# One transfer for the first x and for y of step 6, six stores for the first result, and row sums moved between VectorE and ScalarE, in a softmax over the diagonal of a Gram matrix

## The chip, the core and the metric

The kernel runs on one core of a Trainium2 chip. The metric is the device time of one execution in microseconds, given as the median of several runs.

## The reference

```python
B, N, D = 8, 4096, 512           # x and y: float32, standard normal
gram = np.matmul(x, y.transpose(0, 2, 1))
diag = np.diagonal(gram, axis1=1, axis2=2)      # (8, 4096)
diag = diag - diag.max(axis=-1, keepdims=True)
exp = np.exp(diag)
return exp / exp.sum(axis=-1, keepdims=True)
```

Only the diagonal of the Gram matrix is used, so what is computed is one dot product of 512 elements for each of 8 x 4096 rows, x[b, n] with y[b, n], and a softmax over the 4096 of each batch. No matrix product is needed. The inputs are 2 x 67.1 MB, the output is 131 KB.

## The kernel before

**Tiling.** Four batches at a time fill the 128 partitions: each batch takes 32 partitions, and each partition holds 128 consecutive rows of it. So there are two sets of results, set 0 (batches 0 to 3) and set 1 (batches 4 to 7), each 128 x 128. A set is worked off in four steps of 32 rows per partition, which makes eight steps, t = 0 to 7. One step brings 8 MB of x and 8 MB of y (64 KB of each per partition). In this text x2 is the x of step 2, y6 the y of step 6, and so on.

**Buffers.** `xs` has two buffers (steps alternate), `ys` has one, `side` is a small tile for 6 rows of y. `diag` receives the dot products, `res` the softmax.

**Order.** The schedule is written by hand (`manual_schedule`): each engine carries out its instructions in the order of the code. All loads are issued by SP on one DMA queue (`load_x`, L63, and `load_y`, L66), x of a step ahead of y of that step. An issue waits until the readers of the buffer it overwrites are done. The built program gives the completions of its transfers eight semaphores in turn; an issue also waits, where that is still open, for the transfer eight places ahead of it, which had the same semaphore.

**Steps 0 to 5.** When y has landed, ScalarE copies its last K = 6 rows to `side` (L123), while VectorE multiplies the first 26 rows of x by y in place (`products`, L70, 128x13312). At the end of these two `ys` is free, and SP issues the next y. VectorE then multiplies the last 6 rows with `side` (L70, 128x3072) and adds up the first 30 rows of products in one reduction (`sums`, L73); ScalarE adds up the last W = 2 rows, one ACTIVATE with an accumulator for each (`sums_act`, L78). When all sums of step t are there, its x buffer is free, and SP issues x of step t + 2. In step 0 x comes in two transfers, 2 rows and 30 rows. After step 3 the softmax of set 0 is made (`exps`, `normalize`), its last part at the beginning of step 4.

**Step 6.** x6 comes in one transfer, y6 in two halves of 16 rows. Each half is multiplied (L70, 128x8192) when it is there. ScalarE adds up 24 rows, VectorE 8. `ys` rows 0 to 15 are free after the first product and rows 16 to 31 after the second; y of step 7 goes there.

**Step 7.** x and y come in pieces of 16, 8, 4, 2, 1 and 1 rows, called a to f here (the x of the last two rows comes in one piece, e). VectorE does product and sum of a row in one instruction (`dots`, L83). A maximum over all columns but the last two is taken ahead of the last two rows (`largest`, L97).

**The end.** SP stores set 0 in four pieces of 32 partitions (L156), behind all loads on its queue; the softmax of set 1 follows the last dot product and is stored from ScalarE's queue (L158).

Of the kernel before, what the change touches and what calls it, by code (L numbers as in the profile page):

```python
# [1 line left out]

# [5 lines left out]


@with_exitstack
def kernel(
    ctx: ExitStack,
    tc: tile.TileContext,
    x: bass.AP,
    y: bass.AP,
    out: bass.AP,
):
    nc = tc.nc
    ctx.enter_context(tc.manual_schedule())  # L20
    f32 = mybir.dt.float32
    Alu = mybir.AluOpType
    Act = mybir.ActivationFunctionType
    X = mybir.AxisListType.X
    B, N, D = x.shape
    P = nc.NUM_PARTITIONS
    G = 32
    Q = P // G
    C = N // G
    R = 32  # L30
    H = R // 2
    K = 6
    W = 2
    S = B // Q * (C // R)


    xv = x.rearrange("(s b) (j c) d -> s (b j) c d", b=Q, j=G)
    yv = y.rearrange("(s b) (j c) d -> s (b j) c d", b=Q, j=G)
    ov = out.rearrange("(s b) (j c) -> s (b j) c", b=Q, j=G)

    big = ctx.enter_context(tc.tile_pool(name="big", bufs=1))
    small = ctx.enter_context(tc.tile_pool(name="small", bufs=1))


    xs = [big.tile([P, R, D], f32, name=f"xs{i}") for i in range(2)]
    ys = big.tile([P, R, D], f32, name="ys")
    side = big.tile([P, K, D], f32, name="side")

    diag = [small.tile([P, C + i], f32, name=f"diag{i}") for i in range(B // Q)]
    res = [small.tile([P, C], f32, name=f"res{i}") for i in range(B // Q)]  # L50

    def columns(t, r0, n):
        c0 = t % (C // R) * R + r0
        return slice(c0, c0 + n)

    def rows(t, r0, n):
        return xs[t % 2][:, r0 : r0 + n, :]

    def dots_of(t, r0, n):
        return diag[t * R // C][:, columns(t, r0, n)]  # L60

    def load_x(t, r0, n):
        nc.sync.dma_start(out=rows(t, r0, n), in_=xv[t * R // C, :, columns(t, r0, n), :])  # L63

    def load_y(t, r0, n):
        nc.sync.dma_start(out=ys[:, r0 : r0 + n, :], in_=yv[t * R // C, :, columns(t, r0, n), :])  # L66

    def products(t, r0, n, yt):
        xt = rows(t, r0, n)
        nc.vector.tensor_tensor(out=xt, in0=xt, in1=yt, op=Alu.mult)  # L70

    def sums(t, r0, n):
        nc.vector.tensor_reduce(out=dots_of(t, r0, n), in_=rows(t, r0, n), axis=X, op=Alu.add)  # L73

    def sums_act(t, r0, n):
        for r in range(r0, r0 + n):
            row = xs[t % 2][:, r, :]
            nc.scalar.activation(out=row, in_=row, func=Act.Copy, accum_out=dots_of(t, r, 1))  # L78

    def dots(t, r0, n):  # L80
        for r in range(r0, r0 + n):
            xt = xs[t % 2][:, r, :]
            nc.vector.scalar_tensor_tensor(  # L83
                out=xt, in0=xt, scalar=1.0, in1=ys[:, r, :], op0=Alu.mult, op1=Alu.mult,
                accum_out=dots_of(t, r, 1),
            )

    def over_quadrant(name, column, op, negate=False):

        got = small.tile([P, 1], f32, name=name)  # L90
        nc.vector.tensor_reduce(  # L91
            out=got, in_=column.to_broadcast([P, G]), axis=X, op=op, negate=negate, apply_transpose=True
        )
        return got

    def largest(out, d):
        nc.vector.tensor_reduce(out=out, in_=d, axis=X, op=Alu.max)  # L97

    def exps(i, d):
        mxp = small.tile([P, 1], f32, name=f"mxp{i}")  # L100
        largest(mxp, d)
        nmx = over_quadrant(f"nmx{i}", mxp, Alu.max, negate=True)
        sump = small.tile([P, 1], f32, name=f"sump{i}")
        nc.scalar.activation(out=res[i], in_=diag[i][:, :C], func=Act.Exp, bias=nmx, scale=1.0, accum_out=sump)  # L104
        return sump

    def normalize(i, sump):
        total = over_quadrant(f"sum{i}", sump, Alu.add)
        rc = small.tile([P, 1], f32, name=f"rc{i}")
        nc.vector.reciprocal(out=rc, in_=total)  # L110
        nc.vector.tensor_single_scalar(out=res[i], in_=res[i], scalar=rc, op=Alu.mult)  # L111

    nc.vector.addr_align(128, offset=0, max_nops=0)
    nc.scalar.addr_align(128, offset=0, max_nops=0)

    for t in range(S - 2):
        if t == 0:
            load_x(t, 0, 2)  # L120
        load_x(t, 2 if t == 0 else 0, R - 2 if t == 0 else R)
        load_y(t, 0, R)
        nc.scalar.activation(out=side, in_=ys[:, R - K :, :], func=Act.Copy)  # L123
        if t == C // R:
            normalize(0, sump)
        products(t, 0, R - K, ys[:, : R - K, :])
        products(t, R - K, K, side)
        sums(t, 0, R - W)
        sums_act(t, R - W, W)
        if t == C // R - 1:  # L130
            sump = exps(0, diag[0])

    t = S - 2
    load_x(t, 0, R)
    for r0 in (0, H):
        load_y(t, r0, H)
        products(t, r0, H, ys[:, r0 : r0 + H, :])
    sums(t, R - H // 2, H // 2)
    sums_act(t, 0, R - H // 2)

    t += 1
    r0 = 0
    for n in (16, 8, 4, 2, 1, 1):
        if r0 < R - 1:
            load_x(t, r0, max(n, 2))
        load_y(t, r0, n)
        if r0 == R - 2:
            largest(diag[1][:, C:], diag[1][:, : C - 2])
        dots(t, r0, n)
        r0 += n  # L150

    met = small.tile([P, C - R], f32, name="met")
    nc.scalar.activation(out=met, in_=diag[1][:, : C - R], func=Act.Copy)  # L153

    for p, n in ((0, G), (G, G), (2 * G, G), (3 * G, G)):
        nc.sync.dma_start(out=ov[0, p : p + n, :], in_=res[0][p : p + n, :])  # L156
    normalize(1, exps(1, diag[1][:, C - 2 :]))
    nc.scalar.dma_start(out=ov[1], in_=res[1])  # L158


# [1 line left out]
_INS = ['x', 'y']  # L162
_OUTS = [((8, 4096), 'float32')]


# [23 lines left out]
```

## Time and profile before

| | |
|---|---|
| median of 3 runs | 320.69 us (320.68 to 320.96) |
| span of the profiled execution | 318.9 us |
| busy: VectorE, ScalarE | 244.7 us (77%), 42.0 us (13%) |
| read from HBM, written | 134.22 MB, 0.13 MB |
| mean rate over the span | 421 GB/s |
| products of 26 rows, L70 | 14.03 us |
| products of 6 rows, L70 | 3.35 us |
| products of 16 rows, L70 | 8.68 us |
| sum of 30 rows, of 8 rows, L73 | 16.15 us, 4.42 us |
| one row on ScalarE, L78 | 616 ns, and 186 ns to read the accumulator |
| one row in step 7, L83 | 686 ns, and 81 ns to read the accumulator |

The profile is of one execution. Its span runs from the first to the last instruction, so it is shorter than the measured time, which holds what lies around it. Instruction times are busy times; two neighbours on an engine overlap a little, which is why a row on ScalarE follows the one before it after 0.61 us. Transfers have a time from issue to landing, which includes the wait in the queue behind earlier ones; the records of single DMA packets have start, duration and size.

### The profile page before, as it was taken

The page shows a single profiled execution, that of the slowest core. Times are in us where ns is not written, and L with a number is a line of the kernel's source. Part 1 is how long each engine was busy: PE and PEld are TensorE (multiplying, and loading weights), DVE is VectorE, ACT ScalarE, POOL GpSimd, SP SyncE. Part 2 cuts the span into 40 slices and gives each one's busy share as a digit, 9 for nine tenths or more (in the row PEclk, how much of TensorE's full clock was granted, in tenths as well). Part 3 has the DMA queues.
Part 4 walks back from the last instruction along what each step waited for, and adds up shares of the span by engine and source line. Part 5 has one row for each costly group of instructions (what it writes and reads, how often), then busy time and mean ns, then how long its engine had stood idle before and what let it go on. Part 6 is the DMA issues. An engine that isn't in the chain of part 4 may idle for free.

```text
span 318.9 us, 304 instructions
## 1 busy us (share of the span) xinstructions
DVE 244.7 (77%) x96; ACT 42.0 (13%) x84; POOL 0.2 (0%) x4
## 2 busy tenths in 40 slices
DVE  0000069995899939999399994999949999996995
ACT  1000030100301003010120103000030100197000
POOL 0000000000000000000000000000000000000000
DMA  8989999999999999999999999999999899999993
GB/s 314 493 378 485 436 395 436 485 395 403 510 403 395 477 444 395 427 493 395 403 510 403 395 460 460 395 419 493 403 395 510 358 444 415 444 423 419 421 413 116
DMA packets 4226, 134.37 MB, mean 421 GB/s; under 512 B 512, under 2 KB 768, under 8 KB 1536
## 3 DMA queue, kind: packets, MB, share of 16 engines
q1 hardware_dynamic: 4080, 134.29, 97.8%
q10 hardware_dynamic: 144, 0.07, 0.1%
q14 instruction: 2, 0.02, 0.0%
HBM read 134.22 MB, written 0.13 MB: 421 GB/s over the span
## 4 chain that ended last, share of the span: by engine, by line
DMA 62%; DVE 35%; issue 2%; SPq 0%; ACT 0%; DVEq 0%
DMA ys<-in_y_dram 62%; DVE xs L70 30%; DVE diag L73 4%; DVE xs L83 0%; SPq L63 0%; DVE res L111 0%; DVE nmx L91 0%; DVE sum L91 0%; ACT res L104 0%; DVE rc L110 0%; DVE mxp L97 0%; DVEq L70 0%; SPq L66 0%; DVEq L83 0%
## 5 line engine op out<-in xcount | busy, mean ns | idle before, releaser
L70 DVE TENSOR_TENSOR xs<-xs,ys 128x13312 f32<-128x13312 f32 (+1 forms) x8 | 101.4, 12690 | 66.5 <-DMA ys<-in_y_dram 66.5
L73 DVE TENSOR_REDUCE diag<-xs 128x30 f32<-128x15360 f32 (+1 forms) x7 | 101.3, 14477 | 0.2
L78 ACT ACTIVATE xs<-xs 128x512 f32<-128x512 f32 x36 | 22.2, 616 | 111.0 <-DVE xs L70 111.0
L123 ACT ACTIVATE side<-ys 128x3072 f32<-128x3072 f32 x6 | 16.6, 2764 | 124.0 <-DMA ys<-in_y_dram 124.0
L83 DVE SCALAR_TENSOR_TENSOR xs<-xs,ys 128x512 f32<-128x512 f32 x32 | 19.9, 686 | 3.3 <-DMA ys<-in_y_dram 3.3
L70 DVE TENSOR_TENSOR xs<-xs,side 128x3072 f32<-128x3072 f32 x6 | 20.1, 3351 | 0.0
L78 ACT ACTIVATION_READ_ACCUMULATOR xs<-xs 128x1 f32 x36 | 6.7, 186 | 0.0
L104 ACT ACTIVATE res<-diag,nmx 128x128 f32<-128x128 f32 x2 | 0.8, 402 | 37.6 <-DVE nmx L91 37.6
L83 DVE DVE_READ_ACCUMULATOR xs<-xs,ys 128x1 f32 x32 | 2.6, 81 | 0.0
L123 ACT ACT_TABLE_LOAD x1 | 1.3, 1283 | 1.2 <-PEq L173 1.2
L91 DVE TRANSPOSE_TENSOR_REDUCE sum<-sump 128x1 f32<-128x32 f32 x2 | 0.4, 212 | 1.2 <-ACT res L104 1.2
L111 DVE TENSOR_SCALAR res<-res,rc 128x128 f32<-128x128 f32 x2 | 0.6, 286 | 0.1
L97 DVE TENSOR_REDUCE mxp<-diag 128x1 f32<-128x128 f32 (+1 forms) x2 | 0.4, 220 | 0.1
L91 DVE TRANSPOSE_TENSOR_REDUCE nmx<-mxp 128x1 f32<-128x32 f32 x2 | 0.4, 212 | 0.1
L110 DVE RECIPROCAL rc<-sum 128x1 f32<-128x1 f32 x2 | 0.3, 164 | 0.1
L104 ACT ACTIVATION_READ_ACCUMULATOR res<-diag,nmx 128x1 f32 x2 | 0.4, 186 | 0.0
L97 DVE TENSOR_REDUCE diag<-diag 128x1 f32<-128x126 f32 x1 | 0.3, 284 | 0.1
L153 ACT ACTIVATE met<-diag 128x96 f32<-128x96 f32 x1 | 0.3, 282 | 0.0
L173 POOL MEMSET const-bfloat16-1.0<- 128x1 bf16 x1 | 0.1, 102 | 0.0
L173 POOL MEMSET const-uint8-127<- 128x1 uint8 x1 | 0.1, 102 | 0.0
L173 POOL MEMSET const-float32-0.0<- 128x1 f32 x1 | 0.1, 99 | 0.2 <-issue 0.2
L173 POOL MEMSET const-float32-1.0<- 128x1 f32 x1 | 0.1, 99 | 0.0
## 6 DMA issues: line engine op xcount, KB each, us to landing
ys<-in_y_dram SPq DMA_DIRECT2D x3, 4096.0 KB, 16.0
xs<-in_x_dram SPq DMA_DIRECT2D x1, 7680.0 KB, 21.8
xs<-in_x_dram SPq DMA_DIRECT2D x1, 4096.0 KB, 14.9
xs<-in_x_dram SPq DMA_DIRECT2D x1, 2048.0 KB, 20.5
ys<-in_y_dram SPq DMA_DIRECT2D x1, 2048.0 KB, 17.2
xs<-in_x_dram SPq DMA_DIRECT2D x3, 512.0 KB, 22.1
xs<-in_x_dram SPq DMA_DIRECT2D x1, 1024.0 KB, 19.3
ys<-in_y_dram SPq DMA_DIRECT2D x1, 1024.0 KB, 21.3
```

The costliest lines, as they stand in the source:

```text
L70: nc.vector.tensor_tensor(out=xt, in0=xt, in1=yt, op=Alu.mult)
L73: nc.vector.tensor_reduce(out=dots_of(t, r0, n), in_=rows(t, r0, n), axis=X, op=Alu.add)
L78: nc.scalar.activation(out=row, in_=row, func=Act.Copy, accum_out=dots_of(t, r, 1))
L83: nc.vector.scalar_tensor_tensor(out=xt, in0=xt, scalar=1.0, in1=ys[:, r, :], op0=Alu.mult, op1=Alu.mult, accum_out=dots_of(t, r, 1),)
L91: nc.vector.tensor_reduce(out=got, in_=column.to_broadcast([P, G]), axis=X, op=op, negate=negate, apply_transpose=True)
L97: nc.vector.tensor_reduce(out=out, in_=d, axis=X, op=Alu.max)
L104: nc.scalar.activation(out=res[i], in_=diag[i][:, :C], func=Act.Exp, bias=nmx, scale=1.0, accum_out=sump)
L110: nc.vector.reciprocal(out=rc, in_=total)
L111: nc.vector.tensor_single_scalar(out=res[i], in_=res[i], scalar=rc, op=Alu.mult)
L123: nc.scalar.activation(out=side, in_=ys[:, R - K :, :], func=Act.Copy)
L153: nc.scalar.activation(out=met, in_=diag[1][:, : C - R], func=Act.Copy)
L173: nc = _bacc.Bacc("TRN2", target_bir_lowering=False, num_devices=1)
```

## The change

x0 comes in one transfer of 32 rows, where it came in 2 and 30. In steps 0 to 5 VectorE adds up all 32 rows, ScalarE none. In step 6 y comes in one transfer of 32 rows; ScalarE copies rows 10 to 15 of it to `side`; VectorE multiplies rows 0 to 9 with `ys`, rows 10 to 15 with `side` and rows 16 to 31 with `ys`; ScalarE adds up all 32 rows. Set 0 is stored in six pieces: two of 32 partitions and four of 16.

```diff
-    W = 2
...
     for t in range(S - 2):
-        if t == 0:
-            load_x(t, 0, 2)
-        load_x(t, 2 if t == 0 else 0, R - 2 if t == 0 else R)
+        load_x(t, 0, R)
         load_y(t, 0, R)
...
-        sums(t, 0, R - W)
-        sums_act(t, R - W, W)
+        sums(t, 0, R)
...
     t = S - 2
     load_x(t, 0, R)
-    for r0 in (0, H):
-        load_y(t, r0, H)
-        products(t, r0, H, ys[:, r0 : r0 + H, :])
-    sums(t, R - H // 2, H // 2)
-    sums_act(t, 0, R - H // 2)
+    load_y(t, 0, R)
+    nc.scalar.activation(out=side, in_=ys[:, H - K : H, :], func=Act.Copy)
+    products(t, 0, H - K, ys[:, : H - K, :])
+    products(t, H - K, K, side)
+    products(t, H, H, ys[:, H:, :])
+    sums_act(t, 0, R)
...
-    for p, n in ((0, G), (G, G), (2 * G, G), (3 * G, G)):
+    for p, n in ((0, G), (G, G), (2 * G, H), (2 * G + H, H), (3 * G, H), (3 * G + H, H)):
         nc.sync.dma_start(out=ov[0, p : p + n, :], in_=res[0][p : p + n, :])
```

## The prediction

> **What bounds the kernel now.** First the page: does any engine fill the span, and what does the chain follow?
>
> ```profile
> span 318.9 us, 304 instructions
> ...
> DMA  8989999999999999999999999999999899999993
> ...
> DMA ys<-in_y_dram 62%; DVE xs L70 30%; DVE diag L73 4%; DVE xs L83 0%; SPq L63 0%; DVE res L111 0%; DVE nmx L91 0%; DVE sum L91 0%; ACT res L104 0%; DVE rc L110 0%; DVE mxp L97 0%; DVEq L70 0%; SPq L66 0%; DVEq L83 0%
> ```
>
> The 16 DMA engines are at 8 or 9 tenths in every slice but the last. The chain names VectorE for a third, but the issues (third view) show that it follows releases which came early. So second the windows, from one landing of y to another (start:end, length, then busy time of VectorE, ScalarE, GpSimd, clock, DMA share, GB/s):
>
> ```profile
> 42.40:81.10 38.70, 33.45 (x3) 4.05 (x5) 0.00 (x0) 1.00 1.00 434
> 119.80:158.40 38.60, 33.45 (x3) 4.10 (x5) 0.00 (x0) 1.00 1.00 435
> 197.20:235.90 38.70, 33.45 (x3) 4.05 (x5) 0.00 (x0) 1.00 1.00 434
> ```
>
> A DMA share of 1.00 and 434 GB/s in each step: 16.78 MB take 38.7 us, an 8 MB transfer 19.35 us, and VectorE has 5.2 us to spare. The stream of loads is the bound. It gives up time only at its beginning, in a hole, or behind the last landing (y7f at 313.94 us; what follows to the end of the span is 4.9 us). Third, the issues and what they wait for:
>
> ```profile
> 59.79 16.15 DVE L73 TENSOR_REDUCE diag<-xs 128x30 f32<-128x15360 f32 x1
> 76.02 0.33 SPq L63 DMA_DIRECT2D xs<-in_x_dram  x1
> 81.12 14.03 DVE L70 TENSOR_TENSOR xs<-xs,ys 128x13312 f32<-128x13312 f32 x1 [5.18 <-DMA ys<-in_y_dram]
> 95.21 0.33 SPq L66 DMA_DIRECT2D ys<-in_y_dram  x1
> ```
>
> x2 is issued at 76.02 us, when the reduction of step 0 ends, while y1 is on its way until 81.03: a lead of 5.0 us. y2 is issued at 95.21, x2 lands at 100.39: 5.2 us. So the queue never runs empty. Fourth, the beginning, by the transfers issued in the first 3.5 us (KB, us from issue to landing) and by windows:
>
> ```profile
> xs<-in_x_dram SPq DMA_DIRECT2D x1, 7680.0 KB, 21.8
> xs<-in_x_dram SPq DMA_DIRECT2D x1, 512.0 KB, 4.1
> ys<-in_y_dram SPq DMA_DIRECT2D x1, 40.7
> ```
>
> ```profile
> 0.00:1.75 1.75, 0.00 (x0) 0.59 (x1) 0.20 (x4) 1.00 0.00 0
> 1.75:2.25 0.50, 0.00 (x0) 0.50 (x1) 0.00 (x0) 1.00 0.98 229
> 2.25:2.75 0.50, 0.00 (x0) 0.19 (x1) 0.00 (x0) 1.00 0.67 221
> 2.75:3.25 0.50, 0.00 (x0) 0.00 (x0) 0.00 (x0) 1.00 1.14 344
> 309.00:311.00 2.00, 2.00 (x7) 0.00 (x0) 0.00 (x0) 1.00 1.03 412
> ```
>
> The first packet starts at 1.76 us, 1.02 after its issue. From there the two rows of x0 (packets of 4 KB) move at 220 to 340 GB/s although the engines are nearly all busy; packets of the same 4 KB move at 412 at 309 us. The packet records say why: the first 128 took 234 ns on average (from 156 to 655), those near the end 163. The next packets, of 60 KB, start between 3.55 and 4.44 us and take 2.267 us each without one exception. This spread of 0.9 us between the engines stays: first and last of the 16 report a landing 0.9 us apart for every transfer to the end, and a transfer has landed when its last engine has.
>
> **The change part by part.** The sum is made on the span, 318.87 us; the median lies 1.82 above it, taken as unchanged.
>
> *x0 in one transfer.* The engine that ends last gets to its 60 KB packets at 4.44 us. Now each starts at once on packets of 64 KB (8 per engine, 2.42 us each). Engines start between 1.76 and, at the latest, 2.34 us. To have moved 32 KB at the long packets' pace is 32/64 x 2.42 = 1.21 us. The cold delay now falls on one packet per engine and not on eight: the first sixteen 4 KB packets were late by 10 to 365 ns, so 0.07 to 0.37 for the last engine. Its equivalent of 4.44 is then (2.0 to 2.34) + 1.21 + (0.07 to 0.37) = 3.28 to 3.92: a gain of 0.5 to 1.2 us, middle 0.85. I take the middle, as the 60 KB packets beside the slow ones had no delay at all. Outer bounds: 0.07 (only the eight packets less per engine, 9 to 13 ns each: a packet of 32 KB takes 1.217 us, two of them 0.013 more than one of 64 KB) and, on the losing side, rival 3. All later issues hang on landings by fixed times, so the gain reaches the end whole. y0 and x1 are issued 0.46 us earlier on SP behind work for 20 us: nothing.
>
> *y6 in one transfer.* Its halves landed 9.71 and 9.72 us after what was before them, whole transfers take 19.35: 0.08 us gained.
>
> A page of the Trainium skill, "DMA: Bandwidth & Descriptors", section "Anatomy of one DMA", gives each DMA a fixed cost of about 2.0 us. By it two loads less would be worth up to 4 us (an estimate from that page: 316.7 us); the halves of y6 show that in a full queue it is hidden but for 0.08.
>
> *All 32 sums on VectorE, steps 0 to 5.* Slope of L73: (16.15 - 4.42)/22 = 0.533 us a row, so +1.07 us, and x(t+2) is issued 1.07 us later, six times (x2 to x6 and x7a); the lead shrinks from 5.0 to 3.9. The first packets of a next transfer start some 1.4 us ahead of the landing (x7b's at 292.59, y7a lands at 294.04), so 2.5 us remain against the 1.02 from issue to first packet: nothing, with rival 2 as its price. VectorE's spare time shrinks from 5.2 to 4.1, behind step 3 from 3.3 to 2.2. The 12 rows taken from ScalarE were done 14 us ahead of VectorE's: nothing. The product's end, which frees `ys`, doesn't move.
>
> *Step 6.* VectorE waits for all of y6 (274.6 us), where it did the first half from 269.3. Then 10 rows: 8.68 - 6 x 0.534 = 5.48 us, side 3.35, 16 rows 8.68: 17.5 us, to 292.1, when `dots` can start; y7a lands at 294.04. Cover 1.9 us; beyond it every us is a us at the end. ScalarE's copy (2.76) ends at 277.4, ahead of the 10 rows' end at 280.1, where SP issues y7a (before: 278.04) with x7a under way until 284.3: lead 4.2. Behind it on SP x7b; then y7b waits for the last product, 292.1 (before 286.64), needed when x7b lands at 298.9; c, d, e follow in 3 us. Nothing.
>
> *ScalarE's 32 rows.* 0.614 us each: rows 0 to 15 from 280.1 to 289.9, rows 16 to 31 from 292.1 to 301.9. First needed by the maximum at 312.88: 11 us of cover. From 294 on they run beside `dots`, which no row shows; the two 16-row products took 8.68 us with and without sums on ScalarE, so nothing, at most 1% of 13 rows, 0.1 us.
>
> *Six stores.* 31 transfers on SP's queue as before. The two more wait for the semaphores of y7d (311.4) and x7e (312.7); the stores landed 0.18 us apart, so the last at about 315.1, against 318.05 for set 1: nothing; if the cover failed, 0.4.
>
> Sum: -0.85 - 0.08 = -0.93 us: span 317.9, median 319.8.
>
> **The rivals.**
>
> 1. *The start keeps its cost.* The slow packets come from the time, not from the size: then 0.15 us at most is gained, 320.5. For it: they all lie ahead of 4.3 us. Against: 60 KB packets of the same time were not slowed.
>
> 2. *A lead that is too short (slower).* Place: the six later x issues. Price: 6 x (L - 2.5), with L the time from issue to first packet in a busy queue. It decides from L over 2.5. From below L is 1.02, from above 3.55 (5.0 less 1.4, where no hole is seen): up to 6.3 us, 326. Against: the only row there is, 1.02.
>
> 3. *Long first packets are slowed in proportion (slower).* 234/163 on the first packet of 2.42 us: +1.06, which eats the gain, 320.8; on all eight of x0: +8.5, 328. It decides once a second round is hit. Against: again the 60 KB packets.
>
> The Trainium skill's page "DMA: Bandwidth & Descriptors", section "Latency and other measured facts", speaks against the change: streams in lock step at a large power of two between rows lose rate (207 against 214 GB/s at 512 KiB). Here the pitch is 256 KiB, and one transfer brings the engines closer to step; 3% of the stream would be 10 us (an estimate from that page). The 4 KB packets near the end, all at the same offset of their rows, took 163 ns, which shows no such loss.
>
> **How the numbers follow.** About 0.2%, 0.64 us, is what a measurement of this kernel can tell from no change. The forecast, 0.66: 319.5 to 320.2, nearly all of it beyond 0.64, 0.60 faster and 0.06 same. Rival 1, 0.22: same. Rivals 2 and 3, 0.06 each: slower. Faster 0.60, same 0.28, slower 0.12. Range: down to the largest gain, 1.28, and 0.1 of scatter, 319.3; up past rival 1 and the runs' scatter of 0.27 to rival 3's near end, 321.0.
>
> **What would show it.** Right: x0 lands at 21.8 to 22.5 us (before 22.98), y0 by 41.8 (42.33), windows between landings keep 434 GB/s, x issues have a lead of 3.9, `dots` starts at y7a's landing, the end of the loads at 313.0. Wrong: x0 landing at 22.9 (rival 1), or past 23.5 (rival 3); steps of over 38.8 us (rival 2); `dots` starting later than 0.1 us behind y7a.

## The result and the profile after

| | before | changed |
|---|---|---|
| median, 21 runs each | 320.69 us (320.51 to 321.47) | 321.11 us (320.65 to 322.21) |
| ratio to before | | 1.0013, 95% interval 1.0007 to 1.0018 |
| span of the profiled execution | 318.9 us | 319.2 us |

The change costs 0.42 us on the median. That is less than the 0.2% named ahead as what a measurement can tell; with 21 runs the interval is narrower and leaves out 1. The runs also scatter more: over 1.6 us, where those of before lie within 1.0. Forecast were 319.8 us and a range of 319.3 to 321.0.

The page of the changed kernel, first its span and the tenths of the DMA engines:

```profile
span 319.2 us, 287 instructions
...
DMA  9999999999999999999999999999999999999993
```

The stream of loads is still the bound; its first slice shows 9 tenths where it was 8. But a busy engine isn't one that moves bytes at full pace. The transfers issued in the first microsecond (x0 alone; last column: us from issue to landing):

```profile
xs<-in_x_dram SPq DMA_DIRECT2D x1, 22.5
```

x0 is issued at 0.73 us and lands at 23.24, 0.26 later than both its parts did before (22.98). The forecast had 21.8 to 22.5. One trace alone can't tell here: over the traces of all kernels of this text, but for the one with two queues, x0 lands at 22.94 to 23.34 us where it comes in one transfer (ten traces, median 23.14) and at 22.97 to 23.52 where it comes in two (eight traces, median 23.13). Next the windows from landing to landing of y, as before (last two columns: DMA share, GB/s):

```profile
42.60:81.31 38.71, 34.51 (x3) 2.76 (x1) 0.00 (x0) 1.00 1.00 433
81.31:120.13 38.82, 34.51 (x3) 2.76 (x1) 0.00 (x0) 1.00 1.01 432
120.13:158.85 38.72, 34.51 (x3) 2.76 (x1) 0.00 (x0) 1.00 1.00 433
```

The step from y1 to y2 takes 38.82 us where each took 38.7: a tenth is lost in one step of this execution, with a DMA share of 1.01, so hardly as idle time. Now the issues around it:

```profile
60.03 17.22 DVE L72 TENSOR_REDUCE diag<-xs 128x32 f32<-128x16384 f32 x1
77.27 0.33 SPq L62 DMA_DIRECT2D xs<-in_x_dram  x1
81.40 14.02 DVE L69 TENSOR_TENSOR xs<-xs,ys 128x13312 f32<-128x13312 f32 x1 [4.16 <-DMA ys<-in_y_dram]
95.49 0.33 SPq L65 DMA_DIRECT2D ys<-in_y_dram  x1
```

The reduction takes 17.22 us, as worked out; x2 is issued at 77.27, and y1 lands at 81.31: a lead of 4.0 us. The packet records show what a smaller lead does. In this execution 13 of the 16 packets of 64 KB with which x2 begins took longer than 2.45 us, up to 2.81, and 12 of the 16 of x3 (118.4 to 119.8 us), up to 3.51, where those of before took 2.42 without exception. x2 lands 19.43 us behind y1, 0.07 late, but x3 lands 19.36 us behind y2, which is no loss: the five engines that get to x3 last took at most 2.50. A slow packet costs time only where it falls on the engine that ends last. And the first 16 packets of x0 took 2.59 to 3.31, 2.96 on average.

So the landings of this execution are late against before by 0.26 us at x0, 0.34 at x2, 0.40 at y2, 0.44 at x6, and by 0.36 at y6, which gains 0.08; y7f lands at 314.33 instead of 313.94, and the end follows 4.9 us later, as before.

### The profile page after: what moved, and what is told of

It is laid out like the page before. It is cut to its first block, busy times and chain, and to the rows that moved or that the text cites. A ratio compares the mean times of both kernels' runs of the same rounds, so it can differ in the third digit from the quotient of the medians.

```text
span 319.2 us, 287 instructions
## 1 busy us (share of the span) xinstructions
DVE 246.8 (77%) x96; ACT 41.7 (13%) x77; POOL 0.2 (0%) x4
## 4 chain that ended last, share of the span: by engine, by line
DMA 65%; DVE 33%; SPq 1%; issue 1%; ACT 0%; DVEq 0%
DMA ys<-in_y_dram 65%; DVE xs L69 32%; SPq L62 1%; SPq L65 0%; DVE xs L82 0%; DVE res L110 0%; DVE sum L90 0%; DVE nmx L90 0%; ACT res L103 0%; DVE rc L109 0%; DVE mxp L96 0%; DVEq L69 0%; DVEq L82 0%
## 5 line engine op out<-in xcount | busy, mean ns | idle before, releaser
L69 DVE TENSOR_TENSOR xs<-xs,ys 128x13312 f32<-128x13312 f32 (+2 forms) x8 | 98.3, 12291 | 65.9 <-DMA ys<-in_y_dram 65.9
L72 DVE TENSOR_REDUCE diag<-xs 128x32 f32<-128x16384 f32 x6 | 103.3, 17220 | 0.2
L120 ACT ACTIVATE side<-ys 128x3072 f32<-128x3072 f32 x6 | 16.6, 2763 | 187.2 <-DMA ys<-in_y_dram 187.2
L69 DVE TENSOR_TENSOR xs<-xs,side 128x3072 f32<-128x3072 f32 x7 | 23.5, 3351 | 0.0
L77 ACT ACTIVATE xs<-xs 128x512 f32<-128x512 f32 x32 | 19.6, 616 | 4.7 <-DVE xs L69 4.7
L132 ACT ACTIVATE side<-ys 128x3072 f32<-128x3072 f32 x1 | 2.8, 2763 | 36.0 <-DMA ys<-in_y_dram 36.0
L77 ACT ACTIVATION_READ_ACCUMULATOR xs<-xs 128x1 f32 x32 | 6.0, 189 | 0.0
```

The costliest lines, as they stand in the source:

```text
L132: nc.scalar.activation(out=side, in_=ys[:, H - K : H, :], func=Act.Copy)
```

## The experiments

Two theories were set against each other. **S**: the start, x0 in one transfer, makes the loss. **L** (the cause that rival 2 of the prediction names): the lead of the x issues has become too short. Every kernel was timed beside the kernel before on the same chip; the *span* below is the median over the runs of a kernel, given with the median for before in the same job. So that the semaphores stay in step, kernels with 26 loads store set 0 in five pieces (three of 32 partitions, two of 16).

### One part of the change at a time

**x0 alone.**

> The kernel before with x0 in one transfer (and five stores, so that SP still has 31 transfers), nothing else. Theory S (the first packets of 64 KB set the loss: one engine is held up by two slow packets and by a fetch of instructions): all of the loss is here, +0.3 to +0.5 us on the median and a wider scatter than before; x0 lands at 23.1 to 23.5 us. Theory L (the shorter lead of the x issues makes the loss): within 0.1 us of before. The recorded forecast would have been -0.85.

```diff
-        if t == 0:
-            load_x(t, 0, 2)
-        load_x(t, 2 if t == 0 else 0, R - 2 if t == 0 else R)
+        load_x(t, 0, R)
...
```

Measured 320.69 us, ratio 0.9996 (0.9988 to 1.0005), span 318.9 against 319.0, runs within 0.23 us. No loss, and no 0.85 us either: S falls, and with it the first term of the forecast.

**The change with x0 in two parts again.**

> The changed kernel with x0 in 2 and 30 rows again (and five stores). Theory S: the loss is gone, -0.08 us against before (what y6 in one transfer saves), with the scatter of before. Theory L: still +0.1 to +0.4 us, and transfers of steps 1 to 5 that land over 19.37 us after the one ahead.

```diff
-        load_x(t, 0, R)
+        if t == 0:
+            load_x(t, 0, 2)
+        load_x(t, 2 if t == 0 else 0, R - 2 if t == 0 else R)
...
```

Measured 320.95 us (320.52 to 322.49), ratio 1.0011 (1.0001 to 1.0022), span 319.2 against 319.0. The loss and the scatter stay: as L has it.

**The sums alone.**

> The kernel before with all sums of steps 0 to 5 on VectorE, nothing else: x issues 1.1 us later, lead 3.9 us. Theory S: 0.0 us. Theory L: +0.15 to +0.4 us, with slow packets or pauses where the next x begins.

```diff
-    W = 2
...
-        sums(t, 0, R - W)
-        sums_act(t, R - W, W)
+        sums(t, 0, R)
```

Measured 321.17 us (320.77 to 322.52), ratio 1.0018 (1.0007 to 1.0028), span 319.4 against 319.0. This part alone loses as much as the whole change. Its trace, which is of the slowest of the 12 runs (span 320.7), shows the place. Transfers issued from 76 to 79.5 us, and then from 114 to 118 us:

```profile
xs<-in_x_dram SPq DMA_DIRECT2D x1, 23.4
```

```profile
xs<-in_x_dram SPq DMA_DIRECT2D x1, 24.0
```

A transfer that is issued early enough lands one transfer's time, 19.35 us, after the one ahead of it. Issue to landing is then lead plus 19.35: for 3.9 to 4.0 of lead, 23.3 to 23.4. x2 does that; x3, issued at 115.91, takes 24.0. Windows of the same trace around it:

```profile
100.59:119.95 19.36, 15.29 (x1) 0.00 (x0) 0.00 (x0) 1.00 1.03 433
119.95:139.96 20.01, 19.88 (x3) 2.76 (x1) 0.00 (x0) 1.00 0.97 419
139.96:159.28 19.32, 14.64 (x1) 0.00 (x0) 0.00 (x0) 1.00 1.00 434
```

x3 takes 20.01 us behind y2, and x5 and x7a lose 0.24 and 0.83 in the same way. The 16 packets that begin x3 took 2.56 to 3.69 us, 0.57 too long on average. Most of them follow the last packet of y2 at once; the 16 engines together begin only 0.8 us late. So here the time is lost within the packets, far less by a later begin. That in this run three of six issues lose time, each a different amount, fits the scatter of the runs.

**Step 6 alone.**

> The kernel before with step 6 as in the change (y6 in one transfer, all rows summed on ScalarE; five stores), nothing else. Both theories: -0.08 us, as y6 lands 0.08 us sooner after x6; dots starts at the landing of y7a.

```diff
-    for r0 in (0, H):
-        load_y(t, r0, H)
...
-    sums_act(t, 0, R - H // 2)
+    load_y(t, 0, R)
...
+    sums_act(t, 0, R)
...
```

Measured 321.03 us, ratio 1.0007 (0.9998 to 1.0016). That looks like a loss of 0.2, but it doesn't lie between the first and the last instruction: the span is 318.9 against 319.0, the expected gain, while 2.11 us lie outside the span, where it was 1.78 in the kernel before and 1.80 in the changed one.

### The lead made shorter, without the change

**ScalarE keeps its two rows, VectorE works longer.**

> The kernel before, ScalarE still summing 2 rows, but VectorE sums two rows of each step 0 to 5 a second time into a tile that nobody reads (1.2 us more, lead 3.8 us). Theory L: the loss of the run with all sums on VectorE comes back, +0.4 to +1.0 us with runs scattered over more than 1 us. Rival A (it is the missing work of ScalarE, not the lead): 0.0 us.

```diff
+    junk = small.tile([P, 2], f32, name="junk")
...
         sums(t, 0, R - W)
+        nc.vector.tensor_reduce(out=junk, in_=rows(t, 0, 2), axis=X, op=Alu.add)
```

Measured 322.22 us, ratio 1.0040 (1.0027 to 1.0053), span 320.0 against 319.1. Rival A falls: ScalarE works as before, and the loss is there, 0.9 us in the span (2.19 us lie outside it).

**Both.**

> The kernel before with all sums on VectorE and two rows summed twice: lead 2.7 us. Theory L: the loss grows steeply, +3 to +7 us, at each of the six x issues about 1 us. Rival A: as with all sums on VectorE, +0.4 us, since ScalarE's part is the same.

```diff
-    W = 2
...
+    junk = small.tile([P, 2], f32, name="junk")
...
-        sums(t, 0, R - W)
-        sums_act(t, R - W, W)
+        sums(t, 0, R)
+        nc.vector.tensor_reduce(out=junk, in_=rows(t, 0, 2), axis=X, op=Alu.add)
```

Measured 326.35 us, ratio 1.0157 (1.0140 to 1.0175), span 324.3 against 319.1. Its timeline and its windows:

```profile
77.08 1.21 DVE L129 TENSOR_REDUCE junk<-xs 128x2 f32<-128x1024 f32 x1
78.31 0.33 SPq L62 DMA_DIRECT2D xs<-in_x_dram  x1
81.28 14.03 DVE L69 TENSOR_TENSOR xs<-xs,ys 128x13312 f32<-128x13312 f32 x1 [2.99 <-DMA ys<-in_y_dram]
```

```profile
61.84:81.19 19.35, 16.45 (x2) 0.00 (x0) 0.00 (x0) 1.00 1.01 427
81.19:102.43 21.24, 21.12 (x3) 2.76 (x1) 0.00 (x0) 1.00 0.95 407
102.43:121.78 19.35, 14.52 (x2) 0.00 (x0) 0.00 (x0) 1.00 0.99 427
160.49:181.63 21.14, 21.09 (x3) 2.76 (x1) 0.00 (x0) 1.00 0.99 422
```

With a lead of 2.9 us x2 lands 21.24 us behind y1, x4 21.14 behind y3 and x6 21.48 behind y5: 1.8 to 2.1 us lost each. x3, x5 and x7a lose nothing: when x2 lands late, y2 does too, and x3, issued when VectorE is done with step 1, has a lead of 4.8 us again. So three of the six issues are late, not all. Here both kinds of loss are seen. At x2 the 16 engines together begin 6.5 us later than they could, up to 3.8 us behind the issue, and the first packets take up to 3.52 us, 0.64 too long on average.

### The lead given back to the change

**Two rows on ScalarE again.**

> The change with only the sums of steps 0 to 5 undone (VectorE 30 rows, ScalarE 2): x leads are 5.0 us again, x0 and y6 in one transfer and step 6 as changed. Theory L: the loss is gone and what is left are the two small gains of single transfers, -0.1 to -0.2 us against before, runs within 0.4 us of each other. Theory S: +0.3 us as in the change. As the candidate to beat both kernels: 320.6.

```diff
+    W = 2
...
-        sums(t, 0, R)
+        sums(t, 0, R - W)
+        sums_act(t, R - W, W)
```

Measured 321.01 us, ratio 1.0010 (1.0001 to 1.0019). By the time alone this kernel is about as slow as the change. But again 2.11 us lie outside the span; the span is 318.9 against 319.1, where the change has 319.3. In the trace all x from x2 to x6 land 19.34 to 19.36 us after the y ahead of them, two of them here:

```profile
81.07:100.42 19.35, 19.23 (x3) 4.10 (x5) 0.00 (x0) 1.00 1.00 434
119.77:139.11 19.34, 19.22 (x3) 4.10 (x5) 0.00 (x0) 1.00 1.00 434
```

So the loss in the span goes with this one part, and what is left of the change is 0.2 us shorter than before; the time doesn't show it, for the reason seen with step 6. The next kernel shows it in the time too.

**One row** (the same with W = 1).

> The change with 1 row per step summed on ScalarE: x leads of 4.5 us. Theory L: between the change and the change with 2 rows: a span of 319.0 to 319.1 us, few slow first packets. If the lead has a hard threshold between 3.9 and 4.5: 318.9 as with 2 rows.

Measured 320.69 us against 320.68, ratio 1.0000 (0.9991 to 1.0009), span 318.9 against 318.9. The window from the landing of y1 to that of x2:

```profile
81.00:100.35 19.35, 19.22 (x3) 3.49 (x3) 0.00 (x0) 1.00 1.00 434
```

With a lead of 4.5 us nothing is lost at any x, though 7 of the packets that begin x2 were slow by 0.16 to 0.47 us in its trace.

**Three, four and eight rows** (W = 3, 4, 8).

> The change with 3 rows per step on ScalarE: x leads of 5.5 us. Theory L: span 318.8 to 318.9 us. If the 0.3 us outside the span go with 2 rows alone (a matter of how many instructions ScalarE has), the time is 320.6 to 320.7, the best of all; if with step 6 as changed and few sums on VectorE, 321.0.

> The change with 4 rows per step summed on ScalarE: x leads of 6.1 us. Theory L: as with 2 rows or 0.1 us better, -0.1 to -0.3 us, if no third fetch of instructions falls into the stream; with one, 0.2 us worse.

> The changed kernel with ScalarE summing the last 8 rows in steps 0 to 5 (VectorE 24): x issues come 4.3 us sooner than in the change, lead 8.2 us. Theory L (a next x whose issue leads by 3.9 us or less is slow in its first packets): the loss is gone and the scatter too; -0.1 to -0.3 us against before, runs within 0.3 us of each other, no slow packets after the first round. Theory S: still +0.3 us.

Measured 320.94, 320.88 and 320.93 us, ratios 1.0004, 1.0004 and 1.0005, each with an interval that holds 1; spans 319.2 against 318.9, and twice 319.1 against 319.1. No packet that begins one of x2 to x6 is slow by more than 0.06 us any more, but the spans aren't the 318.9 of one and two rows. All three traces have a third fetch of instructions (8 KB, at 318.0, 296.3 and 278.7 us), which the kernels with fewer rows on ScalarE don't have. It doesn't explain the spans: the first comes behind the last load, and the landings next to the other two are late by 0.05 us at most. y7a, whose lead is 4.1 us in these kernels too, lands 0.18, 0.06 and 0.02 us late. The rest is open.

**All sums on VectorE, x in two halves.**

> The change with all sums on VectorE, but in two instructions of 16 rows, and x2 to x6 in two transfers of 16 rows, the first issued 8.6 us sooner (lead about 12 us; the second half is issued at the change's time, 3.9 + 9.7 us ahead of its turn). Theory L: no slow packets at the begin of x2 to x6; five more transfers of 32 KB packets cost 0.08 each, so about +0.2 us with runs within 0.4 us of each other. If it is VectorE's longer sums by themselves that slow the loads: slow packets as in the change, +0.8 us, runs scattered over 1.5 us.

```diff
-        sums(t, 0, R)
+        sums(t, 0, H)
+        sums(t, H, H)
...
+            load_x(t, 0, H)
+            load_x(t, H, H)
...
```

Measured 321.57 us, ratio 1.0028 (1.0017 to 1.0039), span 319.5 against 319.1, 2.06 outside. The windows of the two halves of x2:

```profile
81.18:90.89 9.71, 9.62 (x1) 2.76 (x1) 0.00 (x0) 1.00 1.01 435
90.89:100.61 9.72, 9.72 (x3) 0.00 (x0) 0.00 (x0) 1.00 1.06 458
```

No packet that begins x2 to x6 is slow by more than 0.08 us. The two halves take 19.43 us where a whole transfer takes 19.35, which makes the 0.4 us of five more transfers. VectorE's longer sums by themselves slow nothing. Nor is it the smaller packets (32 KB) that help: in the same trace those that begin y7a, with a lead of 4.1 us, took up to 1.89 us instead of 1.21. Six of the seven runs lie within 0.2 us, the seventh 1.1 above.

### The start

**Nothing else issued beside x0.**

> The kernel before with x0 in one transfer, and ahead of y0 VectorE clears half of ys, so that SP issues y0 and x1 some 3 to 9 us later, while x0 is under way; y0 isn't needed in the queue until 22 us. If the first packets of x0 are slow because the descriptors of y0 and x1 are made at the same time, they take 2.42 us now and all lands 0.5 us sooner: -0.4 us. If a transfer that starts in an empty queue is slow by itself, the first packets stay at 2.6 to 3.3 us: 0.0 us.

```diff
+    nc.vector.memset(ys[:, :H, :], 0.0)
     for t in range(S - 2):
...
```

y0 was issued at 9.97 us. Measured 320.69 us, ratio 0.9995 (0.9986 to 1.0004), span 318.9 against 319.1. The first 16 packets still took 2.75 to 3.36 us: it isn't the transfers behind x0 that slow it.

**Two queues.**

> The kernel before with x0 in one transfer and y0 issued from ScalarE's queue at the same time. If what makes the first packets slow is that one queue is supplied slowly at first, two queues halve it: -0.3 us. If it is the engines or the memory at their start, it stays: first packets late by 0.5 to 0.6 us per engine, 0.0 us.

```diff
...
-        load_y(t, 0, R)
+        if t == 0:
+            nc.scalar.dma_start(out=ys[:, :, :], in_=yv[0, :, columns(0, 0, R), :])
+        else:
+            load_y(t, 0, R)
...
```

Measured 322.10 us, ratio 1.0048 (1.0035 to 1.0061). The first packets took 2.67 to 3.34 us, so the supply of one queue isn't it either. The loss has another cause, and it is once more a lead: x0 and y0 share the engines, y0 lands at 46.37 instead of 42.3, y1 is issued at 60.5, 1.3 us ahead of x1's landing, and comes late:

```profile
61.76:82.45 20.69, 18.08 (x2) 1.34 (x4) 0.00 (x0) 1.00 1.02 437
82.45:101.88 19.43, 19.30 (x3) 4.10 (x5) 0.00 (x0) 1.00 1.00 432
```

The second window says more than that. It is of x2, issued at 79.94 us, 2.5 us ahead of y1's landing, and only 0.08 us are lost there: no engine begins late, and the first packets took at most 2.65 us. With a lead of 2.9 us the run above lost 1.8 to 2.1 us each time. So a short lead is where time gets lost, but the lead alone doesn't set how much; what else does isn't known.

### What gave no answer to its question

**The lead of y7a.**

> The kernel before with step 6 as in the change, but ScalarE copies 8 rows of y6 aside (into rows of the x buffer that are free until x7c), so that VectorE's first product has 8 rows and y7a is issued at 279.1 us, with a lead of 5.5 us where step 6 as changed has 4.1. If the +0.2 us of that step is the lead of y7a (theory L), it turns to -0.08 us here. If it comes from elsewhere in step 6 (ScalarE beside dots, the stores), it stays at +0.2 us.

```diff
...
+    load_y(t, 0, R)
+    L = 8
+    spare = xs[1][:, R - L :, :]
+    nc.scalar.activation(out=spare, in_=ys[:, H - L : H, :], func=Act.Copy)
+    products(t, 0, H - L, ys[:, : H - L, :])
+    products(t, H - L, L, spare)
+    products(t, H, H, ys[:, H:, :])
+    sums_act(t, 0, R)
...
```

Measured 321.04 us, ratio 1.0009 (1.0000 to 1.0017), as with step 6 alone; but span 318.9 against 319.0 and 2.13 us outside. y7a had a lead of 5.1 us. The question was wrongly put: the 0.2 us lie outside the span, and so not in the loads of step 6.

**A candidate.**

> The kernel before with x0 in one transfer and 8 rows summed by ScalarE in steps 0 to 5: x leads of 9.4 us, y leads and step 6 as before. The candidate to beat both kernels. Theory L: no slow packets are left behind the first round, -0.1 to -0.2 us against before, a scatter of at most 0.2 us. If leads of 5.0 us cost nothing already: -0.07 us, as with x0 alone.

```diff
-    W = 2
+    W = 8
...
-        if t == 0:
-            load_x(t, 0, 2)
-        load_x(t, 2 if t == 0 else 0, R - 2 if t == 0 else R)
+        load_x(t, 0, R)
...
```

Measured 320.86 us, ratio 1.0002 (0.9994 to 1.0011), span 319.1 against 319.0. Nothing is won, although x leads by 8.4 us in the trace (9.4 were expected). In its trace the window from the landing of x6 to that of the first half of y6 is longer than the 9.71 us it has elsewhere:

```profile
q14 instruction: 1, 0.01, 0.2%
```

```profile
255.19:265.16 9.97, 9.97 (x1) 1.85 (x7) 0.00 (x0) 1.00 0.99 428
```

The first line is the third fetch of instructions (at 259.18 us, from the queue list of that window): it runs on one of the 16 engines for 0.31 us, the next packet there takes 1.59 us instead of 1.21, and the load is later by 0.26 us.

**Half the partitions.**

> The run with a lead of 2.7 us again (all sums on VectorE, two rows summed twice), but x2 to x6 come in two transfers of 64 partitions each, the first of half as many packets per engine. If what a late x lacks is the time to make all its packets' descriptors, half as many are ready sooner and the loss of 5.3 us shrinks to 3 or less. If it is a fixed delay of the first packets after any issue, it stays at 5 us or more.

```diff
...
-        nc.sync.dma_start(out=rows(t, r0, n), in_=xv[t * R // C, :, columns(t, r0, n), :])
+        for p in (0, P // 2) if 2 <= t < S - 1 else (None,):
+            part = slice(None) if p is None else slice(p, p + P // 2)
+            nc.sync.dma_start(out=rows(t, r0, n)[part], in_=xv[t * R // C, part, columns(t, r0, n), :])
...
```

Measured 432.56 us (429.69 to 446.35), ratio 1.3466 (1.3421 to 1.3510). The trace is of the longest of the six runs. The window from the landing of y1 to that of the first half of x2:

```profile
82.67:102.51 19.84, 19.72 (x3) 2.76 (x1) 0.00 (x0) 1.00 1.02 211
```

4 MB into 64 partitions take 19.84 us, as long as 8 MB into 128, and the 64 KB packets take about 5.1 us instead of 2.42. The transfers themselves became half as fast, and the question about the lead stays unanswered. The other five runs bear it out: they are 103 to 108 us longer than the run with whole transfers, and five loads of 8 MB at half the rate would make 97 (an estimate: 5 x 19.35).

**No version beats the kernel before by more than the measurement can tell.** x0 in one transfer (0.9996, and 0.9995 with y0 late) and the change with one row on ScalarE (1.0000) are level with it.

## Why the prediction was wrong, point by point

- **The bound** was read rightly: the stream of loads, with what happens at its beginning, in it, and behind it. Every gain and loss found lies there.
- **x0 in one transfer, -0.85 us: the step that failed first.** "The cold delay now falls on one packet per engine and not on eight" is wrong. Summed over the first packets, an engine loses 0.60 us on average before, with eight packets of 4 KB, and 0.60 us after, with two of 64 KB. The latest engine also begins later than reckoned, at 2.71 us and not at 2.34. Rival 1 was right that the cost doesn't depend on the size. What spoke against it, the 60 KB packets without delay, came from a second transfer whose turn came 2.4 us or more behind its issue: they showed a transfer with some lead, not the start of a queue. Alone, x0 in one transfer gave -0.1 us, and its interval holds no change. In the profiled execution it even lost 0.26: the engine that ended last had two slow packets and, between them, a fetch of instructions at 5.02 us (0.31 us). Before, this fetch fell among the 4 KB packets, at 2.89 us.
- **y6 in one transfer, -0.08:** right. y6 lands 19.35 us after x6, before 19.43; in the span, step 6 alone gives -0.1.
- **The later x issues, "nothing": the step that failed second, and the one that gave the result its sign.** The 1.07 us, the six places and the lead of 3.9 were right. The 1.02 us from an issue to its first packet was taken for the time that a late issue needs; it is the time of the first packet's begin, not of the data's full pace. In the run with the sums alone, packets that begin 2.4 to 3.6 us after their issue still took up to 1.3 us longer. Rival 2 had the place and the cause, a lead that is too short. Its picture, an empty queue until the first packets come, holds only in part: at a lead of 4.0 us the loss is mostly within packets that begin on time, at 2.9 us engines also begin late, up to 3.8 us behind the issue. And its form, 6 x (L - what is left of the lead), doesn't hold: at leads of 3.9 to 4.3 us the traces show losses from 0 to 0.83 us, at 2.9 us losses of 1.8 to 2.1 at three issues, and in the run with two queues 0.08 at 2.5. No single L gives these. It was given a chance of 0.06 on a row that measured something else. Its sign, a step of over 38.8 us, came in one step of the changed kernel (38.82). The parts measured alone make +0.2 us of span (-0.1 for x0, -0.1 for step 6, +0.4 for the sums), the change +0.4; the difference is less than their intervals, some 0.3 us to each side, can tell.
- **Step 6, ScalarE's rows, six stores:** right but for one thing, the lead of 4.1 us of y7a: in the trace with three rows on ScalarE y7a lands 9.89 us behind x7a instead of 9.71. The products took 5.49, 3.35 and 8.69 us, y7a was issued at 280.63 (280.1, all shifted by 0.4), VectorE waited 2.10 us for y7a, ScalarE's last row ended at 302.4, the last store landed at 315.40 and set 1's at 318.41.
- **What lies outside the span** was taken as unchanged: it was 1.80 us. That held for the change, but not for seven of the experiments.
- **The rules of the Trainium skill's page "DMA: Bandwidth & Descriptors".** The fixed cost per DMA (section "Anatomy of one DMA") hid itself in a full queue, as the row said; the page's 2.0 us is also a fit for DMAs issued from GpSimd, and these loads are issued from SP. A loss from streams in lock step (section "Latency and other measured facts") isn't seen: 433 GB/s in the windows of the change.

That the shorter lead is the cause of the result is shown from both sides: the sums alone bring the loss, as does longer work of VectorE with ScalarE's sums kept; with one or two rows back on ScalarE the span of the change is 318.9, with one row its time is that of before too. How much a short lead costs isn't settled, and neither is what a late transfer, or one in an empty queue, lacks during its first packets; for x0 neither the transfers behind it nor a second queue changed it.

## What to carry to other kernels

When loads are the bound, read issue to landing against lead plus the time of one transfer: a transfer that takes longer than that has lost time, even where the DMA share says 1.00, and a late issue is the first cause to look for (a fetch of instructions was another here). Keep such issues well ahead, here by 4.5 us or more, and take the lead that is needed from a row with a full queue, not from a cold start. For differences under 0.2%, compare spans as well as times, for what lies outside the span can differ between kernels.

## What the runs showed of the hardware

- 64 KB packets that begin an x with 4.0 us of lead mostly begin on time and are slow inside: 2.56 to 3.69 us in the worst case instead of 2.42. With 2.9 us of lead engines begin late as well, 6.5 us over the 16 of them at one x. The first packets in an empty queue are slow by a like amount, 2.59 to 3.31 us.
- The cold start costs an engine about 0.6 us on average, whether in eight packets of 4 KB or in two of 64 KB.
- Transfers into 64 of the 128 partitions ran at 211 GB/s, into all of them at 433.
- A fetch of 8 KB of instructions in a full stream of loads takes 0.31 us on one DMA engine, and the packet behind it is slow by 0.32 to 0.38 us (three traces). One delayed the landing by 0.26 us, the other two by 0.05 or less.
- The time outside the span was 1.76 to 1.81 us in twelve kernels, the two compared among them, and 2.05 to 2.19 in seven others. The kernels differ in their numbers of instructions; what sets it stays open.
